# Half-keys and queries transposed by DMA, modulation pieces moved, and splits reordered, in a two-block transformer kernel

## The chip, the cores and the metric

One core of a Trainium2 chip runs the whole program. The metric is device time in microseconds (us) of one launch; lower is better. TensorE is called PE below, VectorE DVE, ScalarE ACT, GpSimd POOL and SyncE SP, the queue that issues most of the DMA.

## The reference, cut to what matters

Two blocks over 512 tokens of width 1024. The first is differential attention (8 head pairs, q and k normalised by row and scaled by a gain per column) followed by a mixture of 16 experts with two picked per token:

```python
q = rmsnorm(q.reshape(B, T, H, 2, dh), q_gain) * (dh ** -0.5)
k = rmsnorm(k.reshape(B, T, H, 2, dh), k_gain)
...
pd = p[:, :, 0] - lam * p[:, :, 1]
...
x = x + o.reshape(B, T, H * 2 * dh) @ w_out
x = x + hier_moe(rmsnorm(x, norm_ffn[i]), w_group, b_group, w_router, b_router, w_gate, w_up, w_down)
```

The second block is modulated by a condition; of its context only keys and values are used:

```python
sh_x, sc_x, g_x = split(silu(c) @ w_ada + b_ada, 3)
xn = _rms_norm(x, norm_g) * (1.0 + sc_x) + sh_x
cn = _rms_norm(ctx, norm_g) * (1.0 + sc_c) + sh_c
fx_in, fx_gate, qx, kx, vx, nx_gate = _split_proj(xn @ w_in)
qx = _rms_norm(_heads(qx), q_norm_g)
kx = _rms_norm(_heads(kx), k_norm_g)
f_out = _fourier(fx_in, w_four) * silu(fx_gate)
na_out = _neighbourhood_attention(qx, kx, vx, kc, vc, rel_bias) * silu(nx_gate)
x_new = x + g_x * (concatenate([f_out, na_out]) @ w_out)
```

## The kernel before

Matrices are kept as pairs of 16-bit parts, hi and lo. A product is three matmuls (`mm3`, recorded as line L155), and each float32 weight that comes from memory is split by ACT (the hi part) and DVE (the lo part); `hilo` does the same with an activation. `W[...]` and `EW[...]` are such weights, and `piece(n)` splits n quarters of one. Weights land in 18 buffers of 1 MB ("slots"), and SP, which issues loads in program order, stands at a load until its buffer's last reader is done.

**Attention in two halves.** `proj_heads` projects a row tile of queries or keys, normalises it by row (`k1nat` is the second half's), and, after the tiles, `pairs_T` turns it by PE: a transposition into PSUM (`k1p`), and `hilo` with the gain of the row's partition into `kk` (the second half's keys) or its like. Where `turned` is given, the `turn` step takes the transposition's place: a hi/lo split in natural layout and one DMA transposition per row tile, issued by SP. `attention(0)` runs the first half's softmax and takes its filling PE work from `both()`: the second half's projections, and every fourth step a step of `modulated()`. That generator forms the modulation in six pieces of 512 columns: a matmul with the piece of w_ada (`adap`, 16 per piece), a copy by ACT (`ar`), and 4 small matmuls that bring it into columns (`modp`, 8 rows in the trace), and an addition by DVE (`mod`). Pieces 0 to 3 are shift and scale, 4 and 5 the gate g_x, used at the end of block 2. `attention(1)` is filled by the output projection with `wo0s` and `wo1s`, whose `wo` loads SP issues. Outside the stretches written by hand, a scheduler orders the engines' work by priority, and each queue runs in the order that it then has.

**Routing** is written by hand (`route`). For each of four token tiles there are a normalisation, a transposition, `logits(t)` (`lgp`, for the last tile `lgq`), `biased`, and `ranks` (comparisons `ge`, `df`, sums), which give the choice `A16`. `pk` counts choices by triangular matmuls, `rkm` and `se` follow on DVE, and `xgp` is the first matmul of the experts, which gathers tokens. `keep(n)` runs n matmuls whose result is not used (`kept`).

**Experts.** Loop over e: `hidden(e, 0..1)` are the gate and up products (`gu`), `silu` and `gated` give `hx`, `down` gives `yp`, stored in `y_d` by POOL's queue. The splits of the coming experts stand among them. The last two passes are written out by hand (`tail`), together with the first weights of block 2 (`bk`, `bv`), the context rows (`cn0`, `cn1`), and two rows, scale (`aB`) and shift (`bB`), spread over partitions into `AB`. Then a branch for an overfull expert is skipped (L1088), and POOL gathers the experts' results (`fetch`).

**Block 2.** A loop over 8 column tiles turns and projects the context (`context_cols`, cnp, cnT, kc); `combined(t)` adds the two experts' results to x (`XQ`), `row_scale(t)` takes the row's rms by ACT and POOL (`xn0r`), `row_affine(t)` applies AB (`xr`), and `row_flip` transposes for kx. Then vx, qx (turned by PE: `qxp`, with the gain column `g2`, into `qkx`), ng, the Fourier part and the neighbourhood attention (`ns<-kkx,qkx`), and the output. The second block's keys `kkx` are turned by DMA already.

## Time and profile before

| | us |
|---|---|
| median of 3 runs (862.4 to 865.22) | 864.84 |
| the profiled execution | 865.03 |
| its span | 863.3 |
| PE busy in it | 797.0 (92%) |
| DVE busy | 640.4 (74%) |
| ACT busy | 523.2 (61%) |
| POOL busy | 143.3 (17%) |

The busy share is a mean over stages. The stretch 60–290 is attention, 290–302 routing, 302–579 experts, 584–621 context and rows, 621–740 the second block's projections, and the rest Fourier, neighbourhood and output. In the timelines a row is one or several like instructions of an engine in its order; the bracket is the time that the engine stood before it, and what ended that. The mean granted PE clock is 0.978 of full speed.

### The profile page before, as it was taken

How to read it: one execution, taken by the hardware profiler on the slowest of the kernel's cores; microseconds unless marked ns; L12 is line 12 of the kernel's file. 1: busy time of each engine (PE TensorE's matmuls, PEld its weight loads, DVE VectorE, ACT ScalarE, POOL GpSimd, SP SyncE). 2: the span in 40 equal slices, each digit the busy share in tenths (PEclk: the TensorE clock that was granted, in tenths of full speed). 3: DMA queues.
4: the chain of work that ended last, by engine and by line, in shares of the span. 5: the costliest groups of instructions: out<-in, count | busy, mean ns of one | idle time of the engine just before them, and what ended most of it. 6: DMA issues, size and time to landing. Idle time of an engine off the chain costs nothing. (4 is left out here: it accounts for less than half of the span.)

```text
span 863.3 us, 19008 instructions
## 1 busy us (share of the span) xinstructions
PE 797.0 (92%) x7948; PEld 500.2 (58%) x7948; DVE 640.4 (74%) x1108; ACT 523.2 (61%) x847; POOL 143.3 (17%) x131
## 2 busy tenths in 40 slices
PE   5999999799988899999999999889699999999698
PEld 3445445454444587888888787764344445645344
DVE  5755657486995798999999999965966247885742
ACT  5534445364872478888888878775335156789600
POOL 1140120200051500000000000014551302222000
PEclk9999999999999899999999999998899999999999
DMA  9953420446245569999999999946447008776922
GB/s 339 387 212 129 162 98 8 163 147 178 97 152 217 187 209 337 376 392 398 394 396 399 396 394 397 355 152 226 173 119 205 1 1 199 118 203 120 257 75 70
DMA packets 118779, 190.77 MB, mean 221 GB/s; under 512 B 47808, under 2 KB 48321, under 8 KB 118689
## 3 DMA queue, kind: packets, MB, share of 16 engines
q1 hardware_dynamic: 112736, 170.23, 59.4%
q0 software_dynamic: 3744, 12.98, 4.1%
q10 hardware_dynamic: 2208, 6.29, 2.0%
q8 instruction: 64, 1.05, 0.5%
q14 instruction: 27, 0.21, 0.1%
HBM read 165.89 MB, written 12.59 MB: 207 GB/s over the span
## 5 line engine op out<-in xcount | busy, mean ns | idle before, releaser
L155 PEld LDWEIGHTS <-hT 128*128 128x128 f16 x576 | 55.6, 100 | 67.1 <-issue 9.4
L155 PEld LDWEIGHTS <-xnT 128*128 128x128 f16 x456 | 44.4, 98 | 54.8 <-ACT xnT L166 2.8
L155 PEld LDWEIGHTS <-hx 128*96 128x96 f16 x384 | 45.9, 123 | 34.3 <-ACT hx L166 1.2
L522 ACT ACTIVATE z<-z,mx 128x128 f32<-128x128 f32 (+3 forms) x64 | 35.5, 557 | 43.9 <-DVE mx L520 42.1
L987 POOL DMA_DIRECT2D y_d<-y x16 | 8.2, 515 | 258.2 <-ACT y L986 258.2
L155 PE MATMUL xgp<-se,XSh 128*128 128x96 f16 x512 | 45.9, 206 | 0.0
L155 PE MATMUL xgp<-se,XSl 128*128 128x96 f16 x512 | 45.9, 206 | 0.0
L155 PEld LDWEIGHTS <-XSh 128*128 128x128 f16 x512 | 43.8, 98 | 0.5 <-issue 0.5
L155 PEld LDWEIGHTS <-XSl 128*128 128x128 f16 x512 | 43.8, 98 | 0.1
L520 DVE CUSTOM_DVE_ANT_0 z<-s,misc_a 128x128 f32<-128x128 f32 (+3 forms) x64 | 29.9, 483 | 6.0 <-PE s L155 6.0
L155 PEld LDWEIGHTS <-cT 128*128 128x128 f16 x216 | 20.2, 100 | 22.8 <-issue 3.1
L1455 POOL TENSOR_TENSOR late_b<-late_b,misc_b 128x256 f32<-128x256 f32 x24 | 19.0, 813 | 82.9 <-DVE mxn L1458 78.8
L163 DVE SCALAR_TENSOR_TENSOR ring<-zn,ring 128x512 f16<-128x512 f32 x32 | 21.7, 703 | 14.0 <-ACT ring L1461 13.9
L155 PEld LDWEIGHTS <-oT 128*128 128x128 f16 x192 | 17.0, 98 | 21.4 <-issue 4.2
L1460 ACT ACTIVATE zn<-zn,mxn 128x512 f32<-128x512 f32 x32 | 22.8, 714 | 10.4 <-DVE mxn L1458 10.3
L1458 DVE CUSTOM_DVE_ANT_0 zn<-ns,late_b 128x512 f32<-128x512 f32 x32 | 20.8, 682 | 9.4 <-PE ns L155 9.4
L155 PE MATMUL y<-wo0s,oT 128*128 128x512 f16 x96 | 26.2, 381 | 1.4 <-DVE on L574 1.2
L166 ACT ACTIVATE pth<-pt 128x128 f16<-128x128 f32 (+3 forms) x32 | 13.8, 432 | 22.1 <-PE pt L217 21.9
L155 PE MATMUL k<-wk1s,hT 128*128 128x512 f16 x96 | 24.5, 395 | 1.6 <-DVE k1nat L296 1.6
L155 PE MATMUL y<-wo1s,oT 128*128 128x512 f16 x96 | 23.0, 379 | 3.0 <-DVE XP L163 2.2
L155 PE MATMUL s<-kk,qk 64*128 64x128 f16 (+3 forms) x192 | 24.6, 301 | 0.2 <-DVE mx L520 0.2
L155 PE MATMUL kx<-bks,xnT 128*128 128x512 f16 x96 | 22.3, 388 | 2.6 <-ACT xnT L166 2.6
(730 smaller groups left out, 2362.7 us busy)
## 6 DMA issues: line engine op xcount, KB each, us to landing
w_gate<-in_w_gate SPq DMA_DIRECT2D x32, 1024.0 KB, 12.0
w_up<-in_w_up SPq DMA_DIRECT2D x32, 1024.0 KB, 12.3
w_down<-in_w_down SPq DMA_DIRECT2D x32, 1024.0 KB, 11.8
ada<-in_w_ada SPq DMA_DIRECT2D x12, 1024.0 KB, 7.2
y_d<-y POOLq DMA_DIRECT2D x16, 384.0 KB, 6.8
wk<-in_da_w_in SPq DMA_DIRECT2D x4, 1024.0 KB, 13.5
wv<-in_da_w_in SPq DMA_DIRECT2D x4, 1024.0 KB, 9.9
wo<-in_da_w_out SPq DMA_DIRECT2D x4, 1024.0 KB, 8.0
```

What stands on the lines that cost most here:

```text
L155: nc.tensor.matmul(o, lhsT=lhsT, rhs=rhs, start=start, stop=stop)
L163: return nc.vector.scalar_tensor_tensor(o, in0, sc, in1, op0=op0, op1=op1)
L166: nc.scalar.activation(h, src, AF.Copy, scale=scale)
L520: nc.vector.tensor_tensor_reduce(out=z[:, :n], in0=ps[:, :n], in1=master[:, 384 - P * i:], scale=-hsc, scalar=3e38, op0=ALU.add, op1=ALU.m ...
L522: nc.scalar.activation(z[:, :n], z[:, :n], AF.Exp, bias=mx, scale=-1.0, accum_out=sums[:, c, i:i + 1])
L987: nc.gpsimd.dma_start(y_d[e * CAP:(e + 1) * CAP, :], y[:CAP, :])
L1455: nc.gpsimd.tensor_tensor(m[:, :256], pos[j, "b"][:, c * 256:(c + 1) * 256], mask[:, v:v + 256], op=ALU.add)
L1458: nc.vector.tensor_tensor_reduce(out=z, in0=st[j, t][c], in1=m, scale=-ISC, scalar=3e38, op0=ALU.add, op1=ALU.min, accum_out=mx)
L1460: nc.scalar.activation(z, z, AF.Exp, bias=mx, scale=-1.0, accum_out=sums[:, 2 * t + c:2 * t + c + 1])
```

## The change

- The second half's keys are turned by DMA (`turned` in `proj_qkv`); their column gain goes into the gain of the queries, `gq[:, 4:]`.
- Of the modulation, pieces 4 and 5 leave `modulated()`. Their weights are loaded after the first expert's, and their `adap`, `ar` and `modp` run in the routing, where the `keep` calls are removed; `gates_add` stands behind it.
- In the tail, expert 15's gate weight is split ahead of expert 14's down weight; three quarters of `bk` and the spreading of `bB` move behind the branch.
- `combined` and `row_scale` are reordered around `vc`.
- The second block's queries are turned by DMA, with a gain row `g2r` (q gain by k gain by 4). It is loaded by POOL into the place of the router's weights `wr`.

```diff
-    def turn(norm, nat, s, o):
+    def turn(norm, nat, s, o, row=None):
         def go():
             norm()
-            hilo(s[:, :512], s[:, 512:], nat, 64.0)
+            if row is not None:
+                v = nat.rearrange("p (h d) -> p h d", d=64)
+                nc.vector.tensor_tensor(v, v, row[:, None, :].to_broadcast([P, 8, 64]), op=ALU.mult)
+            hilo(s[:, :512], s[:, 512:], nat, 64.0 if row is None else 1.0)
             nc.sync.dma_start_transpose(o, s)
...
-    g2 = const.tile([P, 2], F32, name="g2s")
-    nc.vector.tensor_scalar_mul(g2, S("q2g", 0, 2), 16.0)
-    nc.vector.tensor_scalar(g2[:, 0:1], g2[:, 0:1], g2[:, 1:2], 1.0 / 64.0, op0=ALU.mult, op1=ALU.mult)
+    nc.vector.tensor_tensor(gq[:, 4:], gq[:, 4:], gk[:, 4:], op=ALU.mult)
+    nc.vector.tensor_scalar(gq[:, 4:], gq[:, 4:], 1.0 / 64.0, None, op0=ALU.mult)
...
-                              f"k{hf}", W[f"v{hf}"], every, late, None, 0 if hf else 2)
+                              f"k{hf}", W[f"v{hf}"], every, late, None, 0 if hf else 2,
+                              turned=QK[1][1].rearrange("p v j t -> p (v j) t") if hf else None)
...
-        ada = {n: modulation(n) for n in range(6)}
-        order = (2, 3, 0, 1, 4, 5)
+        ada = {n: modulation(n) for n in range(4)}
+        order = (2, 3, 0, 1)
...
+    gates = {n: View([t.rearrange("p (k n) -> p k n", k=4) for t in load(cols(a["w_ada"], n), f"ada{n}")]) for n in (4, 5)}
+    def gates_mm(n):
+        gp[n] = bank("sc", f"adap{n}")
+        for k in range(KD):
+            j = k % 4
+            mm(gp[n][32 * j:32 * j + 32, :], csil[:, k, :], gates[n][:, k, :], k < 4, k >= 4)
+    def gates_rows(n):
+        gr[n] = sqt(f"ar{n}")
+        nc.scalar.activation(gr[n], gp[n], AF.Copy)
+    def gates_cols(n):
+        gm[n] = bank("sc", f"modp{n}")
+        for q in range(4):
+            mm(gm[n][:, q * 2:q * 2 + 2], gr[n][:, q * P:(q + 1) * P], K("sel"), True, True)
...
-    keep(4)
+    gates_mm(4)
     logits(3)
+    gates_mm(5)
     split_rows(3)
+    gates_rows(4)
     biased(3)
     ranks(3, 4)
     ahead(5)
     pk = bank("sc", "pk")
     for t in range(NT):
         if t == NT - 1:
-            keep(10)
+            gates_rows(5)
+            gates_cols(4)
+            gates_cols(5)
...
-    keep(4)
...
+    gates_add(4)
+    gates_add(5)
...
-    EW[3 * e + 2].piece(4)
-    down(e - 1, None)
-    hidden(e, 1, EW[3 * e + 3])
+    down(e - 1, EW[3 * e + 3])
+    hidden(e, 1, EW[3 * e + 2])
...
-    down(e, W["k"])
-    run_all(spread(lambda k: mod[:, k, 0:1], AB[1], "bB"))
+    down(e, None)
...
     context_cols(1)
+    W["k"].piece(3)
+    run_all(spread(lambda k: mod[:, k, 0:1], AB[1], "bB"))
...
         if k == 5:
             combined(0)
-            row_scale(0)
-        if k == 7:
-            combined(1)
     project_c("vc", 0)
+    combined(1)
+    row_scale(0)
+    combined(2)
     row_scale(1)
     row_affine(0)
-    combined(2)
     combined(3)
...
+    nc.gpsimd.dma_start(S("wr", 0, 128), a["g2rows"])
+    g2r = S("wr", 0, 64)
+    nc.vector.tensor_tensor(g2r, g2r, S("wr", 64, 64), op=ALU.mult)
+    nc.vector.tensor_scalar(g2r, g2r, 4.0, None, op0=ALU.mult)
...
-    run_all(proj_heads(xh, xl, NT, W["q"], lambda j: g2[:, 0:1], qxh, qxl, D2, "qx", W["ng"], KD, late, None, True))
+    run_all(proj_heads(xh, xl, NT, W["q"], None, None, None, D2, "qx", W["ng"], KD, late, None, True,
+                       turned=qkx[0].rearrange("p v j t -> p (v j) t"), row=g2r))
...
-        if t == 0:
-            run_all(late.pop())
```

**SP's queue in attention(0).** Here are its loads, first before, then after; ada is a half of a modulation piece, wo a half of an output weight, XP two quarters of x, kk1 the second half's keys.

```order
29 L195 DMA ada40_1202<-in_w_ada 128x4x512
30 L195 DMA ada41_1203<-in_w_ada 128x4x512
31 L195 DMA ada50_1471<-in_w_ada 128x4x512
32 L195 DMA ada51_1472<-in_w_ada 128x4x512
33 L195 DMA wo00_1969<-in_da_w_out 128x2x1024
34 L195 DMA wo01_1970<-in_da_w_out 128x2x1024
35 L710 DMA XP0_1967<-in_x 128x1x1024 x2
36 L710 DMA XP1_1968<-in_x 128x1x1024 x2
```

```order
26 L195 DMA ada01_772<-in_w_ada 128x4x512
27 L195 DMA ada10_1002<-in_w_ada 128x4x512
28 L195 DMA ada11_1003<-in_w_ada 128x4x512
29 L327 DMA_TRANSPOSE kk1_738<-k1nat0_1108 128x8x128
30 L327 DMA_TRANSPOSE kk1_738<-k1nat1_1188 128x8x128
31 L327 DMA_TRANSPOSE kk1_738<-k1nat2_1368 128x8x128
32 L327 DMA_TRANSPOSE kk1_738<-k1nat3_1460 128x8x128
33 L195 DMA wo00_1912<-in_da_w_out 128x2x1024
34 L195 DMA wo01_1913<-in_da_w_out 128x2x1024
35 L713 DMA XP0_1910<-in_x 128x1x1024 x2
36 L713 DMA XP1_1911<-in_x 128x1x1024 x2
```

The loads of pieces 4 and 5 are gone from here, and four transposes stand ahead of the loads of wo and x, each behind its k1nat.

**DVE's order in the routing, around the last tile.** First before, then after; sm is the tile of small constants, of which `wr` is a part (L1291, L1292 form `g2r`).

```order
478 L163 SCALAR_TENSOR_TENSOR XSl3_2847<-xs3_3025,m3r_3023,XSh_2843 128x1024
479 L163 SCALAR_TENSOR_TENSOR misc_m_2855<-lgq_3061,m3r_3023,sm_82 128x20
480 L854 TENSOR_TENSOR ge_2856<-misc_m_2855 128x80
481 L856 TENSOR_TENSOR ge_2856<-ge_2856,cst_80 128x80
482 L857 TENSOR_TENSOR df_2857<-ge_2856 128x20x4
483 L858 TENSOR_REDUCE misc_m_2855<-df_2857 128x20
484 L163 SCALAR_TENSOR_TENSOR misc_m_2855<-misc_m_2855 128x16
485 L163 SCALAR_TENSOR_TENSOR misc_m_2855<-misc_m_2855,pk_3090 128x64
486 L918 TENSOR_TENSOR se0_3122<-misc_m_2855,cst_80 128x384
```

```order
476 L163 SCALAR_TENSOR_TENSOR XSl3_2798<-xs3_2976,m3r_2974,XSh_2794 128x1024
477 L163 SCALAR_TENSOR_TENSOR misc_m_2806<-lgq_3016,m3r_2974,sm_82 128x20
478 L1291 TENSOR_TENSOR sm_82<-sm_82 128x64
479 L873 TENSOR_TENSOR ge_2807<-misc_m_2806 128x80
480 L1292 TENSOR_SCALAR sm_82<-sm_82 128x64
481 L875 TENSOR_TENSOR ge_2807<-ge_2807,cst_80 128x80
482 L876 TENSOR_TENSOR df_2808<-ge_2807 128x20x4
483 L877 TENSOR_REDUCE misc_m_2806<-df_2808 128x20
484 L163 SCALAR_TENSOR_TENSOR misc_m_2806<-misc_m_2806 128x16
485 L163 SCALAR_TENSOR_TENSOR misc_m_2806<-misc_m_2806,pk_3056 128x64
486 L940 TENSOR_TENSOR se0_3084<-misc_m_2806,cst_80 128x384
```

The two rows that form `g2r` now stand between the last tile's bias and its comparisons.

**DVE's order at the last experts.** First before, then after.

```order
671 L163 SCALAR_TENSOR_TENSOR w_down14s0_8221<-w_down140_7684,w_down14s0_8221 128x1024 x2
672 L163 SCALAR_TENSOR_TENSOR w_down14s1_8226<-w_down141_7685,w_down14s1_8226 128x1024 x2
673 L163 SCALAR_TENSOR_TENSOR w_gate15s0_8286<-w_gate150_7799,w_gate15s0_8286 128x1024 x2
674 L163 SCALAR_TENSOR_TENSOR w_gate15s1_8339<-w_gate151_7800,w_gate15s1_8339 128x1024 x2
675 L163 SCALAR_TENSOR_TENSOR sg14_8147<-gu1_14_8261,sg14_8147 128x384
676 L168 TENSOR_TENSOR hx14_8373<-sg14_8147,hx14_8373 128x384
```

```order
674 L163 SCALAR_TENSOR_TENSOR w_gate15s0_8199<-w_gate150_7763,w_gate15s0_8199 128x1024 x2
675 L163 SCALAR_TENSOR_TENSOR w_gate15s1_8218<-w_gate151_7764,w_gate15s1_8218 128x1024 x2
676 L163 SCALAR_TENSOR_TENSOR w_down14s0_8250<-w_down140_7648,w_down14s0_8250 128x1024 x2
677 L163 SCALAR_TENSOR_TENSOR w_down14s1_8303<-w_down141_7649,w_down14s1_8303 128x1024 x2
678 L163 SCALAR_TENSOR_TENSOR sg14_8111<-gu1_14_8225,sg14_8111 128x384
679 L168 TENSOR_TENSOR hx14_8337<-sg14_8111,hx14_8337 128x384
```

The splits of w_gate15 and w_down14 have changed places.

## Rows read from the trace of the kernel before

**Rows 1.** Stretches: us, then busy us (x instructions) of PE, PEld, DVE, ACT, POOL; clock, DMA share, GB/s.
```profile
150.00:200.00 50.00, 45.12 (x305) 23.35 (x294) 31.98 (x83) 23.61 (x50) 7.28 (x6) 0.97 0.45 139
...
621.00:690.00 69.00, 68.38 (x323) 31.73 (x322) 38.94 (x59) 25.06 (x40) 23.53 (x18) 0.99 0.40 115
```

**Rows 2.** Timeline of PE, 148–173: start us, duration us, operation, [idle before <- releaser].
```profile
148.96 1.92 PE L155 MATMUL adap<-ada,csil 128*32 128x512 f32 x16
...
154.28 0.37 PE L155 MATMUL o<-v,pth 128*128 128x128 f16 x2 [2.81 <-DVE k1nat L296]
...
170.59 1.04 PE L217 MATMUL k1p<-cst,k1nat 128*128 128x128 f32 x8
171.47 0.95 PE L155 MATMUL modp<-cst,ar 128*128 128x2 f32 x8
```

**Rows 3.** Timeline of DVE at 164.
```profile
164.12 0.69 DVE L296 TENSOR_TENSOR k1nat<-k,k13r 128x512 f32<-128x512 f32 x1 [1.25 <-POOL k13r L207]
```

**Rows 4.** DMA issues: out<-in, queue, count, KB each, median us to landing.
```profile
y_d<-y POOLq DMA_DIRECT2D x16, 384.0 KB, 6.8
...
wo<-in_da_w_out SPq DMA_DIRECT2D x4, 1024.0 KB, 8.0
...
dft<-in_dfg POOLq DMA_DIRECT2D x1, 128.0 KB, 5.9
kkx<-kxnat SPq DMA_TRANSPOSE x4, 4.6
...
nyq<-in_nyq POOLq DMA_DIRECT2D x1, 1.0 KB, 1.8
```

**Rows 5.** Timeline of ACT at 178 and at 322.
```profile
177.85 1.14 ACT L166 ACTIVATE wo0s<-wo,wog 128x1024 f16<-128x1024 f32 x1
...
321.74 3.88 ACT L166 ACTIVATE w_up1s<-w_up 128x1024 f16<-128x1024 f32 x4
```

**Rows 6.** Timeline of PE, 293–302.
```profile
293.08 1.07 PE L155 MATMUL lgq<-sm,xT 128*128 128x20 f32 x8 [1.01 <-DVE xT L786]
...
295.52 4.43 PE L155 MATMUL kept<-XSh,ones 128*128 128x512 f16 x10
299.75 0.22 PE L155 MATMUL pk<-misc_m,tri 128*128 128x16 f16 x1
...
301.36 0.21 PE L155 MATMUL xgp<-se,XSh 128*128 128x96 f16 x1
```

**Rows 7.** Timeline of DVE, 296–299.
```profile
296.77 0.24 DVE L854 TENSOR_TENSOR ge<-misc_m 128x80 f16<-128x80 f32 x1
...
297.89 0.17 DVE L163 SCALAR_TENSOR_TENSOR misc_m<-misc_m 128x16 f16<-128x16 f32 x1
```

**Rows 8.** Stretches, columns as in rows 1.
```profile
556.60:561.60 5.00, 5.00 (x77) 4.97 (x78) 3.96 (x5) 4.31 (x5) 0.00 (x0) 0.66 1.05 394
566.60:571.60 5.00, 5.00 (x105) 4.97 (x104) 3.35 (x7) 3.74 (x7) 2.01 (x3) 1.00 0.43 138
583.50:591.00 7.50, 6.51 (x20) 3.05 (x21) 1.96 (x4) 3.78 (x7) 4.76 (x5) 0.56 0.54 172
```

**Rows 9.** Timeline of PE, 553–584.
```profile
553.20 0.26 PE L155 MATMUL gu<-xgh,w_gate15s 128*128 128x96 f16 x2 [1.15 <-DVE w_gate15s L163]
...
573.77 5.54 PE L155 MATMUL yp<-w_down15s,hx 128*96 128x512 f16 x24 [1.05 <-ACT hx L166]
579.15 1.95 PE L155 MATMUL bB<-cst,mod 128*128 128x128 f32 x16
583.54 0.63 PE L217 MATMUL cnp<-cst,ctx 128*128 128x128 f32 x4 [2.45 <-PEq L1089]
```

**Rows 10.** Timeline of DVE at 574 and 603–608.
```profile
573.75 0.56 DVE L168 TENSOR_TENSOR hx<-sg,hx 128x384 f16<-128x384 f32 x1 [0.59 <-ACT hx L166]
...
603.50 0.15 DVE L205 TENSOR_SCALAR xn0u<-xn0ss 128x1 f32<-128x1 f32 x1 [1.22 <-ACT xn0j L213]
...
607.46 0.15 DVE L205 TENSOR_SCALAR xn1u<-xn1ss 128x1 f32<-128x1 f32 x1 [1.28 <-ACT xn1j L213]
```

More of the change, by code (lines that the diff above doesn't have):

```diff
@@ L38, in _table @@
     return t, n
-COLS, NSMALL = _table((("qg", 1), ("kg", 1), ("subln", 1), ("q2g", 1), ("k2g", 1), ("g2", 8), ("cx", 8), ("cc", 8),
+COLS, NSMALL = _table((("qg", 1), ("kg", 1), ("subln", 1), ("g2", 8), ("cx", 8), ("cc", 8),
                        ("bada", 24), ("lam", 256), ("rb", 20), ("wr", 160), ("gffn", 8)))
@@ L317, in project, with proj_heads @@
         return ps
-    def turn(norm, nat, s, o):
+    def turn(norm, nat, s, o, row=None):
         def go():
             norm()
-            hilo(s[:, :512], s[:, 512:], nat, 64.0)
+            if row is not None:
+                v = nat.rearrange("p (h d) -> p h d", d=64)
+                nc.vector.tensor_tensor(v, v, row[:, None, :].to_broadcast([P, 8, 64]), op=ALU.mult)
+            hilo(s[:, :512], s[:, 512:], nat, 64.0 if row is None else 1.0)
             nc.sync.dma_start_transpose(o, s)
         return go
-    def proj_heads(ah, al, n, w, gain, th, tl, desc, nm, nxt, every, late, done=None, dense=False, pop=1, turned=None):
+    def proj_heads(ah, al, n, w, gain, th, tl, desc, nm, nxt, every, late, done=None, dense=False, pop=1, turned=None, row=None):
         nats = []
@@ L340, in proj_heads @@
             if turned is not None:
-                scale.append(turn(scale.pop(), nat, pair[:, 512:].bitcast(F16), turned[:, :, t * P:(t + 1) * P]))
+                scale.append(turn(scale.pop(), nat, pair[:, 512:].bitcast(F16), turned[:, :, t * P:(t + 1) * P], row))
             if nxt:
@@ L633, in modulated @@
     def modulated():
-        ada = {n: modulation(n) for n in range(6)}
-        order = (2, 3, 0, 1, 4, 5)
+        ada = {n: modulation(n) for n in range(4)}
+        order = (2, 3, 0, 1)
         for n in order[:2]:
             next(ada[n])
-        for i in range(6):
+        for i in range(4):
             yield from ada[order[i]]
-            if i + 2 < 6:
+            if i + 2 < 4:
                 next(ada[order[i + 2]])
@@ L646, in block_kernel @@
     qkslot(0)
-    side = Fill(modulated(), 18)
+    side = Fill(modulated(), 12)
     for i, _ in enumerate(proj_qkv(0, 2, None)):
@@ L741, in block_kernel, with gates_add @@
     attention(1, Fill(behind1(), 16), early)
+    gates = {n: View([t.rearrange("p (k n) -> p k n", k=4) for t in load(cols(a["w_ada"], n), f"ada{n}")]) for n in (4, 5)}
+    gp, gr, gm = {}, {}, {}
+    def gates_mm(n):
[10 more added lines that the diff above has]
+            mm(gm[n][:, q * 2:q * 2 + 2], gr[n][:, q * P:(q + 1) * P], K("sel"), True, True)
+    def gates_add(n):
+        nc.vector.tensor_tensor(mod[:, n * 4:n * 4 + 4, :], gm[n][:, :8].rearrange("p (n v) -> p n v", v=2),
+                                S("bada", n * 4, 4)[:, :, None].to_broadcast([P, 4, 2]), op=ALU.add)
     gainB = w4("gainB")
@@ L797, in logits @@
             mm(o, xTs[t][:, k, :], wrg[:, k, :], k == 0, k == KD - 1)
-    def keep(n):
-        ps = bank("mm", "kept")
-        for _ in range(n):
-            mm(ps, ones, XS[0][0][:, :512], True, True)
     route = ExitStack()
@@ L1558, in host_arrays @@
         "subln": f("da_subln")[0][:, None],
-        "q2g": np.tile(f("q_norm_g_2")[0], 2)[:, None],
-        "k2g": np.tile(f("k_norm_g_2")[0], 2)[:, None],
         "g2": colT(f("norm_g_2")[0]),
@@ L1574, in host_arrays @@
         "w_ada": f("w_ada_2")[0], "w_in": f("w_in_2")[0], "w_four": f("w_four_2")[0], "w_out": f("w_out_2")[0],
-        "ctx": f("ctx_2")[0], "nbias": _window(f("rel_bias_2")[0]),
+        "ctx": f("ctx_2")[0], "g2rows": np.ascontiguousarray(rep(np.concatenate([f("q_norm_g_2")[0], f("k_norm_g_2")[0]]))), "nbias": _window(f("rel_bias_2")[0]),
     }
```

## The prediction

> **What bounds the kernel now.** I read the table by stretches first, to see which engine is full where. In the two attention halves TensorE (PE) works 45.12 of the 50 us from 150 to 200, and in the second block's projections 68.38 of the 69 us from 621 to 690 [rows 1]: an instruction taken from PE there shortens the run, less what falls into a wait of PE. Three places are different: the routing at 290–302, the last two experts at 552–579, and the way from the branch to the first kx matmul at 579–621. There PE waits and another engine's chain sets the time; I read their timelines engine by engine. The profiled execution took 865.03 us (span 863.3), beside a median of 864.84, so the sum can be made against 865.0. Runs tell a change from none at about 0.3%, 2.6 us.
>
> **Attention: second-half keys and two modulation pieces.** Removed from PE: the adap matmuls of pieces 4 and 5, two groups of 16 at 1.92 us; two groups of 8 modp matmuls at 0.95; 16 k1p transposes, of which 8 stand from 170.59 to 171.47, so 0.11 each and 1.76 in all [rows 2]. 2 x 1.92 + 2 x 0.95 + 1.76 = 7.5 us. Not all comes back. The adap group at 148.96 stands just ahead of a wait of 2.81 us for k1nat [rows 2]; VectorE (DVE) ends that wait, whatever PE does before it, so these 1.9 us become a longer wait. The keys' row gain isn't needed (it goes into the queries' gain), so ScalarE (ACT) and DVE do a plain hi/lo split where they scaled PSUM before: no difference to speak of.
>
> New is a wait on SyncE's queue (SP). Four transposing DMAs, each waiting for a k1nat, now stand ahead of the loads of wo, x and the second wo. The last k1nat is made at 164.12 [rows 3]; with 0.69 for that row, about as much for each part of the split, and some 1.4 for the transpose's issue (estimate), wo is issued near 167.5. At wo's median of 8.0 us [rows 4] it is there at 175.5. ACT took it at 177.85 [rows 5], and would come 3 to 5 us sooner now (what PE loses before that, and four scalings of k1p less on ACT). So ACT stands 0 to 3 us before wo0s, with the exponentials of the next heads queued behind it; PE feels it where its fill is used up. I take 1. Transposes of this kind landed in 4.6 us elsewhere in this kernel [rows 4], and the second half's scores are far behind: hidden. If they weren't, PE's first scores of that half would wait.
> Sum: -7.5 + 1.9 + 1 = **-4.6**; bounds -2 (half of what is left goes into waits for ACT and DVE) and -6.5 (the 2.81 wait moves forward too).
>
> **The loads of the moved pieces.** 4 MB now go out on SP behind the first expert's weights, ahead of expert 1's, and take four of the 18 buffers that pace SP. So w_up and w_down of expert 1 wait for the buffers that the end of attention gives free: its output products, which are over before the last logits at 293.08 [rows 6]. From there to the split of w_up at 321.74 [rows 5] it is 28.7 us, and both weights, 4 MB, need 10.6 us at 394 GB/s [rows 8]. **0**; what it would cost uncovered is a rival below.
>
> **Routing.** The 18 `kept` matmuls go, which only kept PE at work; adap and modp of pieces 4 and 5 (3.84 + 1.9 us of PE) stand in their place, 16 on each side of the last logits. In the old run the last pk's input was done at 297.89 + 0.17 = 298.06 [rows 7], but ten kept matmuls from 295.52 held PE until 299.75, and xgp started 1.61 us behind at 301.36 [rows 6]. Without them pk starts when its input is there. From the comparison at 296.77 it is 1.29 us to that input, 1.61 to xgp, and two small rows on the DVE are new (0.17 each, as the row at 297.89): xgp at 296.77 + 0.34 + 2.90 = 300.0, **-1.4**, if nothing waits.
>
> But the first of these new rows is a trap. It multiplies the two gains of the second block, and the order puts it between the last logits' bias and that comparison. It waits for a POOL DMA of 64 KB, which writes over the router's weights and so can't start before the last lgq: 293.08 + 1.07 = 294.15 [rows 6]. DVE stands until it lands at L, with the last ranks, pk and xgp behind it: xgp = L + 0.17 + 0.17 + 2.90, and break-even is L = 298.1, a landing after 4.0 us. The POOL queue's nearest rows: 1 KB in 1.8 us, 128 KB in 5.9, 384 KB in a median of 6.8 [rows 4]. 64 KB lie between the first two, and their middle is 3.9. I take 4: **0**, with bounds of -1.4 (1.8 us: no stop) and +2.8 (6.8 us).
> The Trainium skill ("DMA: Bandwidth & Descriptors", section "Anatomy of one DMA — SWDGE (gpsimd) path") gives a fit for such a DMA of about 2.0 us and its bytes over 436 GB/s; by it, as an estimate, 64 KB land in 2.15 us, near 296.3, DVE never stands, and this term would be -1.4. The rows here don't bear it out but for the smallest: 128 KB took 5.9 us where the fit has 2.3.
>
> In this version PE has gaps of over 1 us on both sides of the last pk. After a stop of 2.45 us that ended at 583.54 [rows 9] the granted clock was 0.56 (much of it at 1.2 of 2.4 GHz) from 583.5 to 591; after PE's stops for w_gate15 around 553 it was 0.66, and 77 matmuls took the 5.00 us in which 105 went at 1.00 [rows 8]. That is 1.3 us for the short case, up to 3.3 (7.5 x 0.44) for the long one; some of it falls into later waits of the first experts. I take **+1** (0 to +3.3).
>
> **Last experts.** DVE and ACT now split w_gate of expert 15 ahead of w_down of 14, as the loop does. Before, PE waited for w_gate15 piece by piece (1.15 us for the first) [rows 9]. That wait goes, and what is late next is hx of expert 15: its DVE row at 573.75 [rows 10] is the end of the same list of splits (nothing is taken from it), and PE's last down starts at 573.77 with it [rows 9]. So PE does its share some 4 us sooner and then stands. Only small waits of ACT on PE vanish, 0.5; the longer stop may cost PE its clock in a down of 5.54 us. -0.5 + 1.5 = **+1** (-0.5 to +2.5).
>
> **Behind the branch.** bB's 1.95 us on PE and three bks splits leave the place ahead of the branch; PE waited there 2.45 us for its sequencer [rows 9], a wait that stays. The context loop that follows has room: DVE works 1.96 of 7.50 us at its start [rows 8], and three splits of 1.22 us fit but for some 1 us; bB is PE work, again 2 us, more at a low clock, in a stretch in which PE waits for cnT anyway. Then DVE runs the chain to kx: combined rows, and row_scale, which waited for ACT's squares 1.22 and 1.28 us (603.50, 607.46 [rows 10]). In the new order another combined stands in each of these waits, and they vanish. -1.95 + 1 - 2.5 - 0.5 (the first affine comes ahead of the last two combined) = **-4** (-1 to -5.5).
>
> **Queries by DMA.** 16 qxp transposes go, 0.11 each as k1p [rows 2]. They lie in a stretch that is all PE. The added row gain, split and four transposes end near 697, far ahead of the first neighbour scores behind ng. **-1.8** (-1.5 to -2).
>
> The expert loop, the neighbourhood and Fourier part and the output keep their order: 0.
>
> **Sum:** -4.6 + 0 + 0 + 1 + 1 - 4 - 1.8 = -8.4, so 865.0 - 8.4 = **856.6**.
>
> **The rivals.** *The attention gain turns into waits.* PE is full on average, but ACT and DVE feed its softmax; with less fill, and wo late by 3, only 1 of the 4.6 us comes back: 860.2. Against it: PE's idle share there is a tenth. *The transfer is early.* 64 KB land within 2.5 us, and adap fills PE so well that the clock stays: routing -1.4 where I have +1, so 854.2; with attention at -6.5, 852.3. For it: the 1 KB row's 1.8 us; against: 128 KB took 5.9 [rows 4]. The Trainium skill's fit (same page and section) is for it, and by it I would say 854.2 myself. *The row gain holds DVE long.* Slower by 2.6 needs the routing at +12 instead of +1 (the rest is -9.4): 3.3 of it clock, 8.7 from L, so L = 306.8, 12.7 us after the issue: 867.6. 384 KB, six times the bytes, took 6.8. *Expert 1's weights come late.* It decides if w_up lands after 321.74, that is if its buffers come free some 20 us later than I think; a whole lost transfer of both is 10.6 us: 867. *The tail does nothing:* the time goes to the y transfer and the gather behind it, which my rows don't price; 860.6.
>
> **How the numbers follow.** Forecast, within 2.5 us of 856.6: 0.46. Transfer early: 0.19. Attention into waits: 0.16. Tail nothing: 0.11. Both slower ones: 0.04 and 0.03; 0.01 elsewhere. Faster by over 0.3% (under 862.2) takes the forecast, the early transfer and most of the next two: 0.84. Same 0.09, where attention and tail fail together or the routing costs 6; slower 0.07. Range: low end from an early transfer, attention -6.5 and the tail -5.5: 850; high end from attention or tail failing with the routing near +3.3: 862.5.
>
> **What would show it.** In the new trace: PE's wait for k1nat at 150 longer by up to 1.9; ACT's idle time ahead of wo0s; on DVE the idle time ahead of the 128x64 row, released by DMA, and xgp's start against the stretch's begin; the granted clock behind it; down of expert 15 still behind hx; kx's first matmul some 4 us nearer to the branch. I am wrong if the stretch 60–290 isn't shorter by 3 us, or if expert 1 waits for DMA.

## The result and the profile after

The changed kernel takes 855.42 us (median of 6 runs, 853.35 to 858.72) beside 865.02 of the kernel before on the same chip (6 runs): a ratio of 0.989, interval 0.9862 to 0.9918. Faster by 9.6 us, where 8.4 were forecast; 855.42 lies in the range. The time of the sum is right, but several of its terms are not, and their errors cancel. The execution that was profiled took 857.49 us. Lines of its page (busy time and share of the span; granted PE clock by slices):

```profile
span 855.7 us, 18940 instructions
...
PE 788.8 (92%) x7898; PEld 495.6 (58%) x7898; DVE 642.0 (75%) x1114; ACT 522.0 (61%) x847; POOL 148.7 (17%) x132
...
PEclk9999999999999799999999999999999999999899
```

The table follows one point after another through the run: how many us *earlier* than in the kernel before each of them starts or ends. Every number is a difference of two start times read from the traces. Where a column's number falls from one line to the next, time was lost between the two points. "Last output product of attention" is the last `y<-wo1s` matmul, "last output product" the last matmul of the run. The forecast column adds up the prediction's terms to the same points. "Again" is a second profile of the same kernel on another chip.

```
                                      forecast  changed  again
last output product of attention        4.6       7.6      7.8
last logits                              4.6       7.6      7.8
first xgp (routing done)                 4.6       6.2      6.5
gate product of expert 8                 3.6       3.2      5.0
end of the last down                     2.6       2.4      4.7
last kx                                  6.6       8.1      8.8
first neighbour scores                   8.4      10.1     10.9
last output product                      8.4       7.6     10.6
```

**Attention.** PE's order there was rebuilt. This is PE's timeline around the wait for the third k1nat (compare [rows 2]):

```profile
148.68 0.95 PE L155 MATMUL modp<-cst,ar 128*128 128x2 f32 x8
149.56 0.66 PE L155 MATMUL s<-kk,qk 64*128 64x384 f16 x6
151.76 0.27 PE L155 MATMUL o<-v,pth 128*128 128x128 f16 x2 [1.54 <-DVE k1nat L296]
```

The wait is 1.54 us, shorter and not longer than the 2.81 of before: a modp group stands ahead of it now, not adap, and it ends 2.5 us sooner.

**Routing.** First POOL's issue of the gain row's DMA, then DVE's timeline (compare [rows 7]) and PE's (compare [rows 6]):

```profile
286.66 0.62 POOL L1289 DMA_DIRECT2D sm<-in_g2rows  x1 [1.39 <-PE lgq L155]
```

```profile
288.94 0.23 DVE L163 SCALAR_TENSOR_TENSOR misc_m<-lgq,m3r,sm 128x20 f32<-128x20 f32 x1
292.41 0.23 DVE L1291 TENSOR_TENSOR sm<-sm 128x64 f32<-128x64 f32 x1 [3.25 <-DMA sm<-in_g2rows]
292.56 0.24 DVE L873 TENSOR_TENSOR ge<-misc_m 128x80 f16<-128x80 f32 x1
```

```profile
289.22 2.04 PE L155 MATMUL modp<-cst,ar 128*128 128x2 f32 x16 [0.54 <-ACT ar L758]
293.90 0.17 PE L155 MATMUL pk<-misc_m,tri 128*128 128x16 f16 x1 [2.64 <-DVE misc_m L163]
...
295.17 0.24 PE L155 MATMUL xgp<-se,XSh 128*128 128x96 f16 x1 [0.91 <-DVE se L940]
```

The trap is there. DVE stands 3.25 us for the row, which was issued at 286.66, behind the last logits, and let DVE go at 292.41, 5.75 us later (forecast: 4). The last ranks, the last pk and xgp come behind it, and PE stands 2.64 and 0.91 us on both sides of that pk. The granted clock is low as well; this is the stretch behind xgp (columns as in rows 1):

```profile
295.20:300.00 4.80, 4.80 (x61) 4.80 (x61) 2.74 (x3) 0.49 (x1) 0.00 (x0) 0.50 1.04 387
```

The clock is 0.50 for all of it, its lower level, 1.2 GHz. In the trace it is at 0.50 from 290.9, in the midst of the modp group and ahead of the stop of 2.64 us, to 301.2. The kernel before has such a stretch in its routing too, which the prediction doesn't count:

```profile
294.40:300.80 6.40, 5.53 (x26) 2.23 (x26) 4.01 (x14) 1.51 (x2) 0.00 (x0) 0.50 0.47 152
```

There it ends at 301.0, just ahead of xgp at 301.36, and so it falls on `kept` matmuls, whose result isn't used. In the changed kernel 6.0 us of it lie behind xgp (2.6 in the second profile, where it ends at 297.5), on work that counts: half of that, 3.0 and 1.3, is what the table shows lost from xgp to expert 8, 3.0 and 1.5.

**The experts.** None of PE's largest waits from 295 to 580 is for a DMA (engine, line, what it waited for: us in total, times, longest):

```profile
PE yp L155 <- ACT hx L166: 5.1, 2, 3.7
PE gu L155 <- issue: 1.4, 1, 1.4
PE gu L155 <- DVE w_gate14s L163: 1.2, 2, 0.7
```

The split of w_up of expert 1 starts on ACT at 318.45, where it started at 321.74 before. The 1.4 us of "issue", at 321.18 in expert 1, is a stop for nothing that the profile names; it isn't in the kernel before, and its cause stays open. The lead is only 1.1 us at the first gate product of expert 2 and 3.2 again at that of expert 8.

**Last down and branch.** PE's timeline (compare [rows 9]):

```profile
569.71 7.23 PE L155 MATMUL yp<-w_down15s,hx 128*96 128x512 f16 x24 [3.74 <-ACT hx L166]
577.24 0.63 PE L217 MATMUL cnp<-cst,ctx 128*128 128x128 f32 x4 [0.30 <-PEq L1111]
577.71 1.95 PE L155 MATMUL bB<-cst,mod 128*128 128x128 f32 x16
...
583.12 0.81 PE L155 MATMUL kc<-bks,cnT 128*128 128x512 f16 x3 [2.82 <-ACT AB L694]
```

hx of expert 15 still starts the last down; PE stands 3.74 us for it and then takes 7.23 us for what took 5.54. The branch costs 0.30 us (PEq is PE's sequencer) and not 2.45. And a new wait stands at 583.12, 2.82 us for ACT's copies of bB.

**Rows of x.** DVE's timeline (compare [rows 10]):

```profile
594.41 5.12 DVE L163 SCALAR_TENSOR_TENSOR XQ<-yg,misc_m,XQ 128x1024 f32<-128x1024 f32 x4
599.44 0.15 DVE L205 TENSOR_SCALAR xn0u<-xn0ss 128x1 f32<-128x1 f32 x1
599.50 2.60 DVE L163 SCALAR_TENSOR_TENSOR XQ<-yg,misc_m,XQ 128x1024 f32<-128x1024 f32 x2
```

Both waits for ACT are gone: a further combined row, two instructions, stands in the place of each.

**Queries.** The new transposes (us to landing, least, median, most) land in 3.1 us, and the first neighbour scores start 2.0 us nearer to the end of qx than before.

```profile
DMA to landing us min/median/max: 3.0/3.1/3.1
```

### The profile page after: what moved, and what is told of

The parts are those of the page before. It is cut to its first block, busy times and chain, and to the rows that moved or that the text cites. A ratio compares the mean times of both kernels' runs of the same rounds, so it can differ in the third digit from the quotient of the medians.

```text
span 855.7 us, 18940 instructions
## 1 busy us (share of the span) xinstructions
PE 788.8 (92%) x7898; PEld 495.6 (58%) x7898; DVE 642.0 (75%) x1114; ACT 522.0 (61%) x847; POOL 148.7 (17%) x132
## 3 DMA queue, kind: packets, MB, share of 16 engines
q8 instruction: 63, 1.03, 0.5%
## 5 line engine op out<-in xcount | busy, mean ns | idle before, releaser
L155 PE MATMUL xgp<-se,XSh 128*128 128x96 f16 x512 | 48.3, 211 | 0.9 <-DVE se L940 0.9
L155 PE MATMUL xgp<-se,XSl 128*128 128x96 f16 x512 | 48.3, 211 | 0.0
L155 PEld LDWEIGHTS <-XSl 128*128 128x128 f16 x512 | 45.6, 101 | 1.0 <-issue 1.0
L155 PEld LDWEIGHTS <-XSh 128*128 128x128 f16 x512 | 45.6, 101 | 0.7 <-issue 0.7
L1486 ACT ACTIVATE zn<-zn,mxn 128x512 f32<-128x512 f32 x32 | 22.8, 714 | 10.5 <-DVE mxn L1484 10.3
L1008 ACT ACTIVATE y<-yp 96x512 f32<-96x512 f32 x32 | 18.7, 586 | 9.1 <-PE yp L155 9.1
L155 PE MATMUL v<-wv1s,hT 128*128 128x512 f16 x96 | 23.9, 399 | 0.0
L155 PE MATMUL z<-bo0s,cT 128*128 128x512 f16 x96 | 22.8, 384 | 1.1 <-DVE fg L163 1.1
```

The source lines that it names most:

```text
L155: nc.tensor.matmul(o, lhsT=lhsT, rhs=rhs, start=start, stop=stop)
L1008: nc.scalar.activation(y[:CAP, cs], ps[:CAP, :], AF.Copy, scale=1.0 / (HS * SW))
L1486: nc.scalar.activation(z, z, AF.Exp, bias=mx, scale=-1.0, accum_out=sums[:, 2 * t + c:2 * t + c + 1])
```

## The experiments

Each changes one thing, against the changed kernel unless it is said otherwise, and was timed in alternation with the kernel before. Ratios are to the kernel before; single ratios here are known to some 0.3%, so that a difference of 1 to 2 us between two kernels is read from the traces (the same points as in the table above) and only supported by the times.

**The gain row's DMA.** The row goes where the lambda vectors were, dead since the run's first 60 us, and its DMA and both rows on the DVE move there:

```diff
-    nc.gpsimd.dma_start(S("wr", 0, 128), a["g2rows"])
-    g2r = S("wr", 0, 64)
-    nc.vector.tensor_tensor(g2r, g2r, S("wr", 64, 64), op=ALU.mult)
+    nc.gpsimd.dma_start(S("lam", 0, 128), a["g2rows"])
+    g2r = S("lam", 0, 64)
+    nc.vector.tensor_tensor(g2r, g2r, S("lam", 64, 64), op=ALU.mult)
```

> The changed kernel with one difference: the gain row is loaded into the place of the lambda vectors, which are dead after the first 60 us, so that its DMA goes out there and the two rows on the DVE leave the routing. Theory 1 (the wait is the price of the routing): the 3.25 us stop ahead of the 128x64 row goes, xgp starts near 8.9 us ahead of the kernel before instead of 6.2, and as PE's stop ahead of the last pk shrinks from 2.64 us to under 1, the clock stays at full, so that the experts run 7 to 8.5 us ahead instead of 3.2; the run is 3.5 to 5 us shorter than the changed kernel, near 851. Theory 2 (DVE and ACT pace the first experts with their splits and give it back): experts still 3 to 4.5 us ahead by expert 3, the run within 1.5 us of the changed kernel.

Ratio 0.9874 (0.9841 to 0.9906), 853.35 us. PE in the routing, and the clock behind xgp:

```profile
286.96 1.95 PE L155 MATMUL modp<-cst,ar 128*128 128x2 f32 x16 [0.54 <-ACT ar L758]
288.77 0.17 PE L155 MATMUL pk<-misc_m,tri 128*128 128x16 f16 x1
...
290.04 0.24 PE L155 MATMUL xgp<-se,XSh 128*128 128x96 f16 x1 [0.91 <-DVE se L940]
```

```profile
290.00:293.00 3.00, 2.96 (x38) 2.96 (x38) 2.26 (x2) 0.21 (x1) 0.00 (x0) 0.50 1.03 398
293.00:298.00 5.00, 5.00 (x89) 4.97 (x88) 2.68 (x5) 2.93 (x5) 0.00 (x0) 0.74 1.04 386
```

The stop is gone. The routing gains 1.5 us on the kernel before (9.8 ahead at the last logits, 11.3 at xgp), where the changed kernel lost 1.4: 2.9 us are the price of the stop, as theory 1 has it. Its second half falls: the clock is at 0.50 from 288.8 to 295.6, behind xgp all the same, and the experts run 8.6 ahead, 2.7 lost again. The shares of attention differ too (below), and by the ratios the gain is 0.1 to 0.2%, which the spread doesn't resolve. The DVE stop is shown by the trace; that it made the clock fall is refuted, here and by the changed kernel itself, where the fall comes ahead of PE's stop.

**PE kept at work behind pk.** As the last, with four matmuls of `keep` back:

```diff
     for t in range(NT):
         mm(pk[:, 64:64 + NE], ones, A16[:, t, :], t == 0, t == NT - 1)
+    keep(4)
```

> As rows_early, with four matmuls whose result is not used put back behind the last pk, where PE otherwise stands until the first xgp. If the clock fell in the changed kernel because of PE's stop ahead of the last pk, which is gone here and in rows_early, the granted clock behind xgp is 1.00 in both, and this run is the same as rows_early within 0.5 us. If the stop of about 1 us behind pk is enough by itself, rows_early shows 0.50 behind xgp and this run doesn't, and this one is 1.5 to 2.5 us shorter.

Ratio 0.9866 (0.9828 to 0.9903), 850.88 us. The clock, columns as before:

```profile
288.70:290.00 1.30, 1.30 (x12) 0.53 (x11) 0.96 (x3) 0.00 (x0) 0.00 (x0) 0.50 1.02 419
290.00:293.00 3.00, 3.00 (x47) 2.67 (x46) 2.09 (x2) 0.32 (x1) 0.00 (x0) 0.69 1.02 391
293.00:298.00 5.00, 4.93 (x115) 4.79 (x113) 3.99 (x6) 4.13 (x6) 0.00 (x0) 1.00 1.05 388
```

xgp itself comes 0.4 us later than without the four (10.9 ahead), but the clock is back at 1.00 from 291.8, where the run without them is at 0.50 until 295.6, and the experts run 10.0 ahead: 1.3 us better, of which attention brings 0.3. So the stop of under 1 us behind pk isn't what makes the clock fall (here it fell at 288.4, ahead of the place of that stop, with PE busy; its last stop before was one of 0.54 us ahead of modp). How long it stays low does go with the four matmuls: 1.3 us of the low stretch lie behind xgp here and 1.7 in early_keep_bk, the other kernel that has them, against 2.6 to 6.0 in the nine profiles that have adap in the routing and not these four. In all eleven, what is lost from xgp to expert 8 is half of that time, within 0.3 us. But the same kernel's two profiles differ by 3.4, so that the length isn't the kernel's alone.

**Modulation pieces.** As rows_early, with pieces 4 and 5 back in attention and all 18 `keep` matmuls back in the routing:

```diff
-        ada = {n: modulation(n) for n in range(4)}
-        order = (2, 3, 0, 1)
+        ada = {n: modulation(n) for n in range(6)}
+        order = (2, 3, 0, 1, 4, 5)
...
-    gates_mm(4)
+    keep(4)
     logits(3)
-    gates_mm(5)
...
-            gates_rows(5)
-            gates_cols(4)
-            gates_cols(5)
+            keep(10)
...
+    keep(4)
```

> As rows_early, but modulation pieces 4 and 5 are back in the first attention half and the 18 unused matmuls are back in the routing; the keys by DMA stay. Theory 1 (PE's work counts one to one in attention): the last output product of attention comes 5.7 us later than in the changed kernel (2 x 1.92 + 2 x 0.95), that is 1.8 to 2 us ahead of the kernel before instead of 7.6; the routing takes what it took before; the run near 856 to 857 is 5 to 6 us longer than rows_early. Theory 2 (the pieces filled waits for k1nat): 2 to 4 us later only, the run 2 to 4 us longer than rows_early.

Ratio 0.9925 (0.9896 to 0.9954), 857.91 us, 4.6 us over rows_early. Attention ends 1.0 us ahead of the kernel before, against 7.6 to 10.1 with the pieces moved. Against rows_early that is 8.9 us later. At the 32nd of the 64 exponentials (ACT's `z<-z,mx`), up to which the clock is full in both from 60 us on, it is 4.6 later, with one modp group of 0.95 still to come: 5.5 of the 5.7 us of PE work, as theory 1 has it. The rest is clock: behind that group it is at 0.50 from 198.2 to 205.0. The wait that adap was thought to fill is here, with the pieces back,

```profile
152.62 0.27 PE L155 MATMUL o<-v,pth 128*128 128x128 f16 x2 [1.44 <-DVE k1nat L296]
```

1.44 us, as short as without them. So it isn't the leaving of the pieces that shortened this wait; DVE stood there for POOL, 2.50 us in the kernel before and 1.57 here, and why POOL came sooner isn't shown.

**Keys.** The second half's keys by PE again:

```diff
-                              f"k{hf}", W[f"v{hf}"], every, late, None, 0 if hf else 2,
-                              turned=QK[1][1].rearrange("p v j t -> p (v j) t") if hf else None)
+                              f"k{hf}", W[f"v{hf}"], every, late, None, 0 if hf else 2)
...
-    nc.vector.tensor_tensor(gq[:, 4:], gq[:, 4:], gk[:, 4:], op=ALU.mult)
-    nc.vector.tensor_scalar(gq[:, 4:], gq[:, 4:], 1.0 / 64.0, None, op0=ALU.mult)
```

> The changed kernel with the second half's keys turned by PE again, all else as changed. Theory 1: 16 transposes come back, 1.8 us at the last output product of attention (5.8 ahead of the kernel before instead of 7.6), and the run is 1.5 to 2 us longer than the changed kernel. Theory 2 (the DMA turn also took work off ACT and DVE, or its wo loads come too late): over 3 us longer, or shorter by some tenths if the late wo was costing more than the transposes.

Ratio 0.9911 (0.988 to 0.9943), 856.24 us. Attention ends 7.0 ahead, 0.6 to 0.8 less than in the two profiles of the changed kernel. The two differ in more than the keys: in the changed kernel the clock fell for some us at 164, which costs 1.6 us (12 matmuls of v in 4.31 us instead of 2.76), and here it didn't. The same stretch in the changed kernel and in rows_early:

```profile
164.00:168.00 4.00, 4.00 (x21) 1.69 (x19) 1.96 (x8) 1.92 (x6) 0.00 (x0) 0.58 1.05 340
```

```profile
164.00:168.00 4.00, 4.00 (x26) 2.14 (x27) 2.58 (x9) 2.63 (x7) 0.00 (x0) 1.00 0.97 354
```

But keys_by_pe has a low stretch that the changed kernel lacks, from 230.7 to 234.1, and its lead falls by 1.5 us there, so that the two cancel, and the ends show 0.6 to 0.8 for the keys, the times 0.2%. Without low clock in either, rows_early and keys_by_pe can be compared from the 26th exponential to the 50th (170.7 to 226.0 in the kernel before), which takes in the transposes: rows_early gains 4.8 us there on the kernel before, keys_by_pe 2.9. The 1.9 between them bear out theory 1's 1.8. The late load of wo shows where the clock didn't fall, in rows_early on ACT:

```profile
168.77 1.15 ACT L166 ACTIVATE wo0s<-wo,wog 128x1024 f16<-128x1024 f32 x1 [0.74 <-DMA wo<-in_da_w_out]
```

0.74 us, inside the 0 to 3 of the prediction; in the changed kernel itself ACT came later, and didn't stand.

**The same kernel once more.**

> The changed kernel once more, as the base for the next three runs on the same chip. If the fall of the granted clock at 164 to 168 and the loss of 2.6 us behind 800 belong to the first profiled execution alone, this profile doesn't have both of them, attention's last output product is 7.5 to 10 us ahead of the kernel before and the end about 10; if they belong to the kernel, the profile shows both again and the end is 7.6 ahead.

Ratio 0.9882 (0.9836 to 0.9928), 855.04 us. The fall of the clock at 164 is there again, and in old_splits; the other seven kernels with the same attention don't show it, and five of those have one at 193 to 195 instead. Attention ends 5.8 to 10.1 us ahead of the kernel before in these ten profiles. The loss behind the neighbour scores is 0.3 here and not 2.5; the others lose 0.2 to 2.0 there.

**The order of the last splits.**

```diff
-    down(e - 1, EW[3 * e + 3])
-    hidden(e, 1, EW[3 * e + 2])
+    EW[3 * e + 2].piece(4)
+    down(e - 1, None)
+    hidden(e, 1, EW[3 * e + 3])
```

> The changed kernel with the splits of w_gate of expert 15 and w_down of expert 14 in their old order, all else as changed. Theory 1 (the new order only gathers PE's stops into one of 3.7 us ahead of the last down, which costs the clock in it): PE waits piece by piece for w_gate15 again, the last down takes 5.5 us instead of 6.9 to 7.2 and ends 0.9 us earlier or more against the experts ahead of it; the run is 0.5 to 2 us shorter. Theory 2 (the slow last down is what hides PE's wait at the branch, 0.30 instead of 2.45 us): the wait at the branch comes back to 2 us or more, and the run is the same or up to 1.5 us longer.

Ratio 0.9864 (0.9817 to 0.991), 853.96 us. PE's timeline:

```profile
548.65 0.26 PE L155 MATMUL gu<-xgh,w_gate15s 128*128 128x96 f16 x2 [1.14 <-DVE w_gate15s L163]
...
570.20 5.54 PE L155 MATMUL yp<-w_down15s,hx 128*96 128x512 f16 x24 [1.04 <-ACT hx L166]
576.07 0.63 PE L217 MATMUL cnp<-cst,ctx 128*128 128x128 f32 x4 [0.33 <-PEq L1112]
```

PE waits for w_gate15 again, the last down takes 5.54 us, and the branch costs 0.33: theory 2 falls, the slow down isn't what hides the branch. But from expert 8 to the end of the last down this kernel loses 1.0 us on the kernel before, and the changed one 0.8 and 0.3. The order moves PE's stops and the clock about, and is worth nothing that these runs show.

**The shift row's place.** bB and three quarters of bk ahead of the branch again:

```diff
-    down(e, None)
+    down(e, W["k"])
+    run_all(spread(lambda k: mod[:, k, 0:1], AB[1], "bB"))
...
-    W["k"].piece(3)
-    run_all(spread(lambda k: mod[:, k, 0:1], AB[1], "bB"))
```

> The changed kernel with the spreading of the shift row and three quarters of bk ahead of the branch again; combined and row_scale stay in the new order. Theory 1 (the place of bB sets PE's wait at the branch): 1.95 us of PE and the wait of 2.45 us come back ahead of the first context transposition, the context loop gets 1 us back, and the run is 3 us longer. Theory 2 (the wait at the branch has to do with the long last down alone): only the 1.95 us come back and 1 us goes, the run is 1 us longer or the same.

Ratio 0.9881 (0.9834 to 0.9927), 854.85 us. PE:

```profile
574.04 1.95 PE L155 MATMUL bB<-cst,mod 128*128 128x128 f32 x16
578.36 0.63 PE L217 MATMUL cnp<-cst,ctx 128*128 128x128 f32 x4 [2.37 <-PEq L1112]
```

The wait of 2.37 us is back, so the place of bB sets it, as theory 1 says. But the run is not 3 us longer: between the end of the last down and the last kx the gain on the kernel before is 4.0 us here and 4.1 in the same-chip profile of the changed kernel. What the branch gives, 3.7 us, the context loop takes back: bB's own 1.95 us stand in it, with the wait of 2.73 for ACT's copies, and only a wait of 0.95 for cnT goes.

**Combined rows.** `combined` and `row_scale` in their old order around vc:

```diff
         if k == 5:
             combined(0)
+            row_scale(0)
+        if k == 7:
+            combined(1)
     project_c("vc", 0)
-    combined(1)
-    row_scale(0)
-    combined(2)
     row_scale(1)
     row_affine(0)
+    combined(2)
     combined(3)
```

> The changed kernel with combined and row_scale in their old order around vc; the spreading stays behind the branch. Theory 1 (row_scale's waits for ACT were on the path): two waits of DVE of 1.2 to 1.3 us come back near 598 and 601, the first kx matmul starts 2.5 to 3 us later against the end of the context loop, and the run is 2.5 to 3 us longer. Theory 2 (the gather from memory is what comes last): no change within 0.5 us at kx.

Ratio 0.9933 (0.9905 to 0.9961), 858.57 us, 3.5 us over the changed kernel on the same chip. DVE:

```profile
592.83 2.60 DVE L163 SCALAR_TENSOR_TENSOR XQ<-yg,misc_m,XQ 128x1024 f32<-128x1024 f32 x2
596.64 0.16 DVE L205 TENSOR_SCALAR xn0u<-xn0ss 128x1 f32<-128x1 f32 x1 [1.22 <-ACT xn0j L213]
...
600.60 0.15 DVE L205 TENSOR_SCALAR xn1u<-xn1ss 128x1 f32<-128x1 f32 x1 [1.28 <-ACT xn1j L213]
```

Both waits are back, and between vc and the last kx the gain of 2.7 us on the kernel before is a loss of 0.2. Theory 1 holds: this order is 2.7 of the 4.1 us that the change wins behind the branch in the same-chip profile.

**bk ahead, bB behind.** Following from spread_ahead, the three splits go back under the last down, where ACT and DVE have room, and only bB stays behind the branch:

```diff
-    down(e, None)
+    down(e, W["k"])
...
-    W["k"].piece(3)
     run_all(spread(lambda k: mod[:, k, 0:1], AB[1], "bB"))
```

> The changed kernel, but the three quarters of bk are split under the last down again, and only the spreading of bB stays behind the branch. Theory 1 (with bB and bk behind the branch the gain of 3.7 us at the branch is lost again to PE's wait of 2.7 to 2.8 us for the copies that ACT makes behind three splits): PE's wait at the branch stays under 0.6, the wait for AB in the context loop goes, vc's last matmul comes 2 us earlier against the last down, and the run is 1.5 to 2.5 us shorter than the changed kernel. Theory 2 (the gather of the experts' results, or DVE's chain behind it, comes last anyway): vc earlier, but the first kx at the same place, and the run within 0.5 us.

Ratio 0.9842 (0.9811 to 0.9873), 851.43 us. PE:

```profile
574.85 0.63 PE L217 MATMUL cnp<-cst,ctx 128*128 128x128 f32 x4 [0.45 <-DVEq L1111]
575.32 1.95 PE L155 MATMUL bB<-cst,mod 128*128 128x128 f32 x16
577.10 1.51 PE L155 MATMUL kc<-bks,cnT 128*128 128x512 f16 x6
578.46 0.38 PE L217 MATMUL cnp<-cst,ctx 128*128 128x128 f32 x2
```

The branch costs 0.45 us, the wait for the copies is gone, and kc starts right behind bB. From the end of the last down to the last vc 5.7 us are gained on the kernel before, against 2.9 and 1.4 in the two profiles of the changed kernel, and the neighbour scores come 14.7 ahead. 2.8 us of that are the wait; the second profile had its clock low from 580.8 to 584.2 besides. Theory 1 holds, with more than it forecast: by the ratios 0.4%, some 3.5 us, though on another chip and with intervals that overlap.

**All three corrections.**

> The changed kernel with the three corrections together: gain row loaded early, four unused matmuls behind the last pk, bk split under the last down. If they add (3 to 4 us of the routing and 2 behind the branch), the run is near 849.5 and 1.6% faster than the kernel before; if the gain behind the branch is swallowed by the gather, it is like rows_early_keep, 1.35% faster.

Ratio 0.9813 (0.9781 to 0.9846), 849.31 us: the gain row early, the four matmuls of `keep` behind pk, and bk ahead of the branch with bB behind it. It is the fastest version, 1.9% ahead of the kernel before and some 6 us ahead of the changed one. By the ratios the first two are worth 0.2% on the changed kernel, bk 0.4, and all together 0.7 to 0.8: they add up, within what single ratios tell. In this profile attention ends only 5.8 ahead, with a clock of 0.90 from 180 to 230, so that the times and not this profile's end tell what the three are worth.

**Queries by PE.** The second block's queries by PE, with the gain column and no gain row at all (`turned` and `row` left out of that call of `proj_heads`).

> The changed kernel with the second block's queries turned by PE and scaled by a gain column again; no gain row is loaded at all. It tells two things. Theory 1: without the row the routing's stop of DVE goes, as in rows_early (xgp some 1.4 us nearer to the last logits), and the turn costs 1.8 to 2.0 us between the end of qx and the first neighbour scores; the two nearly cancel, and the run is within 1.5 us of the changed kernel. Theory 2 (the stop of DVE is not due to the row's DMA): xgp where it was, the run 2 us longer.

Ratio 0.9895 (0.9861 to 0.993), 856.24 us. The routing gains 1.2 us on the kernel before instead of losing 1.4, and from the end of qx to the first neighbour scores nothing is gained where the changed kernel gains 2.0. Theory 1: the stop was due to the row's DMA, and in this change the turn of the queries paid for itself barely, since it brought that row.

## Why the prediction was right, point by point

That 855.4 came so near to 856.6 is in part luck: attention gave 3 us more than forecast, and the routing with its clock took some 2 to 3 more.

- **What bounds the kernel.** Right in both places where PE is full: work taken from it there came back whole or nearly (5.5 of 5.7 for the pieces, 1.9 of 1.8 for the keys, 2.0 of 1.8 for the queries).
- **Attention: 4.6 forecast, 7.6 and 7.8 measured; the term was mis-sized.** The 7.5 us of PE work were right. The step that failed is the 1.9 that I took off because adap "stands just ahead of a wait of 2.81 us". I held the order and the wait of before fixed. The scheduler rebuilt the order, and the wait got shorter, 1.54 us, and 1.44 with adap back ahead of it; what shortened it stays open. How near 7.6 is to 7.5 is chance: the same attention ended 5.8 to 10.1 ahead, as the clock fell. Also the 1 us for wo: at most 0.74 of ACT, and none of it seen at PE.
- **Loads: 0 forecast**, and no DMA is among PE's waits of the experts.
- **Routing: 0 and +1 forecast; 1.3 to 1.4 to xgp and 1.5 to 3.0 from there to expert 8.** The trap, its place and its chain were right; its size was short: L was 5.75 us after the issue and not 4, inside the bounds. By the fit of the Trainium skill ("DMA: Bandwidth & Descriptors", section "Anatomy of one DMA — SWDGE (gpsimd) path"), 2.15 us as an estimate, DVE would not have stood at all; the measurement decides against it here, with the DMA engines at a share of 1.03 in this stretch. I interpolated by bytes and left the load of the DMA engines out: in the kernel before, 256 KB of the same queue (`late_b`) took 7.2 us at a share of 1.08 and 3.0 at 0.27. The clock term, +1 with bounds of 0 to 3.3, measured 1.5 to 3.0, and its cause was wrong: I took the clock as full in the old routing and low because of the new gaps. It was at 0.50 there too (the ten `kept` matmuls of [rows 6] took 0.44 us each, the four at 290.24 only 0.26), and it falls ahead of the stop. What changed is how much of the low stretch lies behind xgp.
- **Last experts: +1 forecast, 0.3 to 0.8 measured.** The new wait, its length (3.74) and the slow down behind it came as described. But the old order loses as much in the new surroundings, so the term is not the order's.
- **Behind the branch: 4 forecast, 5.7 and 4.1 measured; the sum right, two of its parts wrong.** "A wait that stays" failed: the sequencer's wait goes with bB (2.45 to 0.30, 0.56 in the second profile). "Fit but for some 1 us" failed the other way: the splits and the copies behind them stop PE for 2.8 us. The two cancel, as spread_ahead shows. The combined rows, 2.5 and 0.5 forecast, gave 2.7.
- **Queries: 1.8 forecast, 2.0 measured.**
- **The rest: 0 forecast**, 0.3 lost in the second profile, 2.5 in the first.

Put together for the second profile: 8.4 forecast, + 3.2 in attention, − 1.8 in routing and up to expert 8, + 0.7 in the last experts, + 0.3 behind the branch and in the queries, − 0.3 in the rest, makes 10.5, the 10.6 of the table but for rounding. Of the rivals, "attention into waits" and "transfer early" are both refuted by the trace; so are "expert 1's weights come late" (its split of w_up starts 3.3 us sooner than before) and "the tail does nothing" (5.7 and 4.1 us). The long hold of DVE would have needed 12.7 us from the issue, and it was 5.75.

## What to carry to other kernels

A wait next to a removed instruction is no price as long as a scheduler may move what stands there; cost the removed work at full, and keep the wait as a bound. A small constant that reuses a dead buffer inherits the buffer's last reader: look for the place whose reader is longest done, since the in-order engine behind that load stands for all. And when work moves past a branch, move only what isn't needed to fill the engines on its near side: bB alone behind the branch was worth some 3 us more than bB with the splits (2.8 of it the wait of PE that went).

Matmuls that only keep PE at work didn't keep the clock up in the old routing; they took the low stretch upon themselves. Look where a low stretch ends, and what stands in it, in the kernel before as well, and not only whether the clock falls.

## What the runs showed of the hardware

- PE's stop at a branch whose body is skipped was 2.37 and 2.45 us in the two profiles with bB's 16 short matmuls ahead of it, and 0.30 to 0.56 in the eleven with the last down directly ahead, be it fast (5.54 us) or slow (up to 8.12). That the place of bB sets it is shown by spread_ahead and bk_ahead. My reading of why, not shown: with bB ahead the sequencer reaches the branch late, and without it does the branch's work under the down. The Trainium skill ("Runtime: NRT & Kernel Launch", section "Instruction fetch mechanics") says that a taken branch to a target outside the fetched pages makes the engine fetch it by DMA before it goes on. The traces don't decide whether the stop is such a fetch: two instruction packets (0.03 MB) move from 570 to 585 with the long stop and with the short one. The first of them starts 1.0 us behind the end of the last down in the two profiles with the long stop, and 2.4 to 3.8 us ahead of it in the changed kernel's two, old_splits and bk_ahead, which is in keeping with my reading; which engine they are for isn't told.
- The clock fell to its lower level, 0.50, in rows_early_keep at 288.4, and PE was busy from there through 290, behind a stop of 0.54 us and, ahead of that, some 6 us of adap and lgq; a full PE in the profile isn't the same as a clock that stays.
- A POOL DMA of 64 KB took 5.75 us from its issue to its reader in the changed kernel, as long as 128 KB (5.9 in [rows 4]), with the DMA engines at a share of 1.03; it landed within 5.4 to 5.9 in all eleven profiles that have it. Its time goes with the load more than with the size: in the changed kernel's profile 256 KB by the same queue (`late_b`) took 5.6 us at a share of 1.04 and 2.8 at 0.32.
